# The recurrence's 128x128 transposes as 32x32 blocks on VectorE, moved into place by ScalarE, in a one-layer RWKV-7/Conformer step

## Chip, cores and metric

The kernel runs on one core of one Trainium2 chip. The metric is the device time of one execution in microseconds (us). The kernel before was run three times: median 1765.64 us, from 1764.25 to 1766.26. The profile is one more execution, 1765.73 us, of which 1763.5 us lie between its first and its last instruction (the span).

The five engines are called PE (TensorE; PEld is its weight load), DVE (VectorE), ACT (ScalarE), POOL (GpSimd) and SP (SyncE, which here only starts transfers). Each works through its own list of instructions in order.

## What is computed

One inference step of a hybrid decoder layer for 520 tokens (512 of one prompt, 8 single decode tokens), all in fp32. Cut to what matters:

```python
proj = rmsnorm(x, norm_g) @ w_in              # 2048 -> 3200 + 1024 + 2048 + 1024 + 4096 columns
r, k, v, ... = token_shift(proj)              # 16 heads of 64
def step(S, inp):                             # the recurrence, one token at a time
    sa = einsum('bhij,bhj->bhi', S, a_t)
    S = S * w_t + sa[..., None] * b_t + v_t[..., None] * k_t
    return S, einsum('bhij,bhj->bhi', S, r_t)
o = group_norm(scan(step)) + bonus
y_a = (o * silu(gate_a)) @ w_proj_a
y_b = (silu(layer_norm(conv31(glu))) * silu(gate_b)) @ w_proj_b
h = x + (sigmoid(ga) * y_a + sigmoid(gb) * y_b) @ w_out
h = h + sigmoid(h @ w_ple_gate) * (p @ w_ple)
y = rmsnorm(h, final_g)
```

## The kernel before

**The matrix products.** Activations lie as 128 channels by 520 tokens. Each weight and each activation is split into two fp32r parts, high and low, and a product is three matmuls (high-high, high-low, low-high), each in two halves of 260 tokens. `step` (L196 to L213) issues these six matmuls for one 128x128 weight. Weights are prepared in slabs of four such steps: ACT rounds the high part `wh` (L154, 128x512), DVE subtracts to get the low part `wl` (L67). Both have four buffers (`WB = 4`), and `step` asks for slabs up to three ahead (`AHEAD = 3`). So the rounding of slab k can start when PE has finished slab k-4, and PE needs it three slabs later. One slab is 24 matmuls.

**The order of the work.** The order on PE and DVE is the order in which the program issues. After each step, `tick` (L174) advances every running generator, and `yield n` means "go on n steps later". A generator that yields ROOM waits until a model of DVE's time (`work`, L95, with the charges of L103) has not run more than 1 us ahead of PE's. The order on ACT, POOL and SP is made at build time by a scheduler, which takes instructions as they become ready in its own model, in the order of issue where several are ready. Every engine then keeps its fixed order on the chip.

**The recurrence.** `wkv(p, box)` is a generator for head pair p, eight of them. Pair p+1 prepares its operands while pair p runs its scan. Its stages:

- `bk` (the decayed b and k of the pair) is multiplied with `ar`, giving the masked matrices `nba` and a part of `bn`. Then `bk` itself is transposed: 8 blocks of 128x128 in two groups of four, on PE against an identity (L548 to L551), and ACT copies each group of four out of PSUM into `bn` with one instruction.
- a 32x32 triangular inverse on DVE, whose blocks go into `ttb` (ACT, L615 and L617, 32 partitions each).
- `v` is transposed: four blocks on PE (L621 to L626), copied into `suv` by four ACT instructions. The scan starts from `suv`.
- the scan over eight chunks of 64 tokens. Each chunk has three groups of small matmuls on PE, `ly = 4` steps, one slab, apart: first `ar` x `suv` (called y here), copied by ACT to `xs` (L642); then `ttb` x `xs` (z), copied by ACT to `suv` (L648); then `bn` x `suv`, after which DVE computes the next chunk's `suv` and ACT scales it to `sf` (L662). Each group needs the copy behind the group before it.
- the group norm of the output `oc`; its normalised `on` is transposed, four blocks on PE (L693), and DVE multiplies straight out of PSUM into `og` (the buffer `bv`, L697), writing the pair's output.

**The end.** The last product is split into token halves. `finish` (L1050) sums the squares, takes root and reciprocal (`rf`), and multiplies all 16 blocks `h2[j]` by it, each group followed by its transfer to `y`. In the second half, which nothing follows, DVE multiplies 12 blocks in four instructions and POOL the blocks 12 to 15, one by one; transfers of DVE's groups are started by ACT, those of POOL's by SP.

Of the kernel before, what the change touches and what calls it, by code (L numbers as in the profile page):

```python
# [11 lines left out]
AF = mybir.ActivationFunctionType  # L12
ALU = mybir.AluOpType
# [4 lines left out]
P = 128  # L18
T = 520
NPR = 512  # L20
NS = 8
HF = T // 2
# [13 lines left out]


GROUPS = ([range(2 * _g, 2 * _g + 2) for _g in range(8)],
          [range(0, 1), range(12, 13), range(1, 4), range(4, 8), range(13, 16), range(8, 12)])
ON_POOL = (12, 13, 14, 15)  # L40


M_R, M_K, M_V, M_L, M_GA, M_GLA, M_GLB, M_GB, M_SA, M_SB = 0, 8, 16, 24, 25, 33, 41, 49, 57, 73
# [8 lines left out]
ROOM = -1  # L52
# [18 lines left out]
def body(nc, tc, a):  # L71
    with ExitStack() as es:
# [21 lines left out]
        act = nc.scalar.activation  # L94
        clock = {"pe": 0.0, "dve": 0.0}  # L95

        def work(us):
            clock["dve"] = max(clock["dve"], clock["pe"]) + us
# [1 line left out]
        def pe_work(name, n):  # L100
            clock["pe"] += 0.13 if n > 32 else 0.04

        vec = Paced(nc.vector, lambda name, n: work(0.0069 * n if name == "reciprocal" else (0.2 if name == "scalar_tensor_tensor" else 0.14) + 0.00107 * n))  # L103
        gps = Paced(nc.gpsimd, lambda name, n: work(0.0014 * n if n > 64 else 0.05))
        pe = Paced(nc.tensor, pe_work)

        def tt(eng, out, x, y, op):
            eng.tensor_tensor(out, x, y, op=op)
# [106 lines left out]
        def gemm(nk, xs, hs=(0, 1)):  # L215

            o = pm.tile([P, 2, 512], F32, name="mm")
            for k in range(nk):
                step(k, nk, xs[k], [o[:, h, :HF] for h in range(2)], hs)
                tick()  # L220
            return o[:, :, :HF] if len(hs) == 2 else o[:, hs[0], :HF]
# [6 lines left out]
        def half(h):  # L228
            return slice(64 * h, 64 * h + 64)

        def quarter(i):
            return slice(32 * i, 32 * i + 32)
# [19 lines left out]
        o = pa.tile([P, 512], F32, name="aux", tag="aux")  # L252
# [27 lines left out]
        ident = cst[:, C_ID:C_ID + P]  # L280
# [14 lines left out]
        def aux(name="aux"):  # L295
            return pa.tile([P, 512], F32, name=name, tag="aux")
# [43 lines left out]
        for i, n, o in ((0, 252, first[3][0]), (252, 252, first[3][1]), (504, 16, first[2][0])):  # L340
            o = o[:, HF:HF + n]
# [12 lines left out]
        def gt(name):  # L354
            return gp.tile([P, T], F32, name=name, tag="g")
# [71 lines left out]
        def wkv(p, box):  # L427
# [25 lines left out]
            for j, (out, off) in enumerate(((sg, O_W0), (av, O_A0))):  # L453
                for h in range(2):
                    hs = slice(h * HF, (h + 1) * HF)
                    o = aux()
# [45 lines left out]
            v = box["v"]  # L502
# [9 lines left out]
            bk = kq.tile([P, NCH, 2, 64], F32, name="bk")  # L512
# [16 lines left out]
            bn = bns[p % 2]  # L529
            f2 = lambda x: x.rearrange("p c a t -> p c (a t)")  # L530
            for c0 in (0, 4):
# [6 lines left out]
                for h in range(2):  # L538
                    s, u, o = half(h), half(1 - h), os[h]
                    mk = lambda s, i, n: gmask[s, i:i + n].unsqueeze(1).to_broadcast([64, 4, n])  # L540
                    tt(vec, nba[s, c0:c0 + 4], o[s, :, h * 64:h * 64 + 64], mk(s, 0, 64), ALU.mult)
                    i = 64 * (1 - h)
# [2 lines left out]
                    yield ROOM  # L545

            for c0 in (0, 4):
                o = aux().rearrange("p (c x) -> p c x", x=P)  # L548
                for c in range(4):
                    pe.transpose(o[:, c, :], f2(bk)[:, c0 + c, :], ident)  # L550
                act(bn[:, c0:c0 + 4].rearrange("p c h a x -> p c (h a) x")[:, :, 0::3, :],  # L551
                    o.rearrange("p c (h x) -> p c h x", h=2), AF.Copy)
                yield 2

            nd = dr.tile([2, NCH, 2, 32, 32], F32, name="nd", tag="nd", bufs=2)
            td = dr.tile([2, NCH, 2, 32, 32], F32, name="td", tag="td", bufs=2)
# [4 lines left out]
            o = aux()  # L561
# [31 lines left out]
            o = aux().rearrange("p (c x) -> p c x", x=64)  # L593
            for c in range(NCH):
                for h in range(2):
                    x, y = quarter(2 * h), quarter(2 * h + 1)
                    pe.matmul(o[y, c, 0:32], lhsT=nba[x, c, 32:64], rhs=dtt[x, c, :], start=True, stop=True)
            yt = kq.tile([P, NCH, 32], F32, name="yt")
            for h in range(2):
                y = quarter(2 * h + 1)  # L600
# [8 lines left out]
            o = aux().rearrange("p (c x) -> p c x", x=64)  # L609
            for c in range(NCH):  # L610
                for h in range(2):
                    x, y = quarter(2 * h), quarter(2 * h + 1)
# [5 lines left out]
            yield 2  # L618

            suv = kq.tile([P, 2, NCH, 64], F32, name="suv")  # L620
            o = aux().rearrange("p (w x) -> p w x", x=P)  # L621
            for w in range(4):
                pe.transpose(o[:, w, :], v[:, w * P:(w + 1) * P], ident)
            for e in range(2):
                for h in range(2):
                    act(suv[half(1 - h), h, e::2], o[half(e), :, h * 64:h * 64 + 64], AF.Copy)  # L626
            gps.memset(suv[0:64, 0, 0, :], 0.0)
            gps.memset(suv[64:128, 1, 0, :], 0.0)
            yield 6
# [3 lines left out]
            for c in range(NCH):  # L633
# [3 lines left out]
                y, z = yy[:, c % 2, 0], yy[:, c % 2, 1]  # L637
# [47 lines left out]
            on = gt("on")[:, :NPR].rearrange("p (c x) -> p c x", x=P)  # L685
# [3 lines left out]
                       m[half(1 - h), 1, e::2].unsqueeze(2).to_broadcast([64, 4, 64]), ALU.mult)  # L689
                yield ROOM  # L690
            yield 5
            ot = aux()
            for c in range(4):  # L693
                pe.transpose(ot[:, c * P:(c + 1) * P], on[:, c, :], ident)
            og = bv[:, :NPR]
            sl = box["sl"]
            yield 1  # L697
# [215 lines left out]
        for p in range(8):  # L913
# [7 lines left out]
            o = gemm(16, xn)  # L921
# [7 lines left out]
            o = gemm(16, xn)  # L929
# [4 lines left out]
            o = gemm(16, xn)  # L934
# [48 lines left out]
        def st(name):  # L983
            return sp2.tile([P, T], F32, name=name, tag="s")
# [11 lines left out]
        for j in range(KD):  # L996
            x = st("x")
# [12 lines left out]
        for k in range(2):  # L1010
            x = st("p")
# [4 lines left out]
        acc, rf = st("acc"), st("rf")  # L1016
        h2 = [hp.tile([P, 4, T], F32, name="h2") for _ in range(4)]
# [34 lines left out]
        def finish(h, sq):  # L1052
            t, sent = tok(h), [None, None]
            while flag["gated"] < LAST + (KD - LAST) * (h + 1):
                yield 1
            yield 4 * (1 - h)
            o = aux()
            nc.tensor.matmul(o[:, :HF], lhsT=one, rhs=acc[:, t], start=True, stop=False)
            nc.tensor.matmul(o[:, :HF], lhsT=one, rhs=sq[:, t], start=False, stop=True)  # L1059
            act(rf[:, t], o[:, :HF], AF.Sqrt, scale=1.0 / 2048, bias=eps[:, 0:1])  # L1060
            yield 14 * (1 - h)
            for i in range(0, HF, 130):
                r = rf[:, t][:, i:i + 130]
                vec.reciprocal(r, r)
                if h == 0:
                    yield ROOM
            for js in GROUPS[h]:

                if h and js[0] not in ON_POOL:
                    y = h2[js[0] // 4][:, js[0] % 4:js[-1] % 4 + 1, t]  # L1070
                    tt(vec, y, y, rf[:, t].unsqueeze(1).to_broadcast([P, len(js), HF]), ALU.mult)
                else:
                    for j in js:
                        y = h2[j // 4][:, j % 4, t]
                        tt(gps if h else vec, y, y, rf[:, t], ALU.mult)
                        if h == 0:
                            yield ROOM
                y = h2[js[0] // 4][:, js[0] % 4:js[-1] % 4 + 1, t]
                q = int(h == 1 and js[0] not in ON_POOL)
                with tc.issue_after(sent[q].ins) if h and sent[q] else ExitStack():  # L1080
                    sent[q] = (dma, nc.scalar.dma_start)[q](out=a["y"][js[0]:js[-1] + 1, :, t].rearrange("a p t -> p a t"), in_=y)

        flag["gated"] = 0
        order.enter_context(tc.manual_schedule(engines={mybir.EngineType.DVE}))
# [2 lines left out]
        for h in range(2):  # L1087
            for j in range(LAST, KD):
                sq = gate(j, (h,))
            start(finish(h, sq))  # L1090
# [74 lines left out]
```

## Time and profile before

| | us |
|---|---|
| median of three runs | 1765.64 |
| the profiled execution | 1765.73 |
| its span | 1763.5 |
| PE busy | 1746.3 |
| DVE busy | 1256.1 |
| ACT busy | 831.7 |
| POOL busy | 154.6 |

A row of a group of instructions reads: line, engine, operation, output <- inputs by the program's names (so `aux` is any PSUM scratch tile), shape, count | busy time, mean duration in ns of one | idle time of the engine just before them. A row of a timeline reads: start, duration, engine, line, operation, names, count. A row of the windows reads: stretch, length, then busy time of PE, PEld, DVE, ACT, POOL with counts, the granted PE clock as a share of full speed, the share of the DMA engines, GB/s. Matmuls overlap, and their ends are modelled; the pace of PE is read from starts.

### The profile page before, as it was taken

Reading aid. Unit: us, or ns where it says so; the run is one execution under the profiler, and the core shown is the slowest. Engines: PE = TensorE matmul, PEld = TensorE weight load, DVE = VectorE, ACT = ScalarE, POOL = GpSimd, SP = SyncE. Lnnn points to the kernel's source line nnn. Section 1 sums busy time; section 2 is a strip of 40 time slices with the busy share of each in tenths; the row PEclk is TensorE's granted clock in tenths of the full one; section 3 lists DMA queues with packets and bytes.
Section 4 is the critical chain, followed back from the end, with each engine's and each line's share of the span. In section 5 each row is a group of like instructions: output and inputs, shape, how many; then the busy total and the mean of one; then the engine's idle time right before and its main releaser. Section 6 shows DMA issues by size and latency. Waiting matters only on the chain.

```text
span 1763.5 us, 36946 instructions
## 1 busy us (share of the span) xinstructions
PE 1746.3 (99%) x15064; PEld 1736.0 (98%) x15064; DVE 1256.1 (71%) x2411; ACT 831.7 (47%) x1644; POOL 154.6 (9%) x205
## 2 busy tenths in 40 slices
PE   9999999999999999999999999999999999999996
PEld 9999999999999999999999999999999999999996
DVE  7578889889888898888898998577344333334557
ACT  6734546456455464474564433455233222243344
POOL 1100100001001001000010000002022000001111
PEclk9999999999999999999999999999999999999998
DMA  7252333333333433334324444568455332353333
GB/s 231 88 128 91 95 115 98 97 109 100 121 92 85 127 100 97 109 93 110 108 86 115 144 133 151 172 223 271 153 186 181 121 110 95 98 190 96 96 100 106
DMA packets 122186, 221.34 MB, mean 126 GB/s; under 512 B 48017, under 2 KB 57361, under 8 KB 122017
## 3 DMA queue, kind: packets, MB, share of 16 engines
q1 hardware_dynamic: 120416, 217.39, 39.9%
q8 instruction: 118, 1.93, 0.5%
q10 hardware_dynamic: 1600, 1.60, 0.3%
q14 instruction: 52, 0.42, 0.1%
HBM read 189.61 MB, written 29.34 MB: 124 GB/s over the span
## 4 chain that ended last, share of the span: by engine, by line
PE 97%; DVE 1%; DMA 1%; ACT 0%; POOL 0%; issue 0%; SPq 0%; POOLq 0%; DVEq 0%; ACTq 0%
PE mm L211 89%; PE aux L67 7%; PE aux L211 1%; DMA w<-in_win 0%; DVE h L67 0%; DMA x<-in_xT 0%; POOL h L67 0%; DVE wl L67 0%; DVE c L67 0%; DVE rf L67 0%; PE aux L1059 0%; POOLq L1161 0%; SPq L143 0%; ACT wh L154 0%; ACT ttb L615 0%
## 5 line engine op out<-in xcount | busy, mean ns | idle before, releaser
L154 ACT ACTIVATE wh<-w 128x512 fp32r<-128x512 f32 (+1 forms) x541 | 338.9, 628 | 603.4 <-PE mm L211 529.3
L211 PE MATMUL mm<-xh,wh 128*128 128x260 f32 x2784 | 581.8, 290 | 0.6 <-ACT xh L266 0.4
L211 PE MATMUL mm<-xh,wl 128*128 128x260 f32 x2784 | 561.1, 283 | 0.0
L211 PE MATMUL mm<-xl,wh 128*128 128x260 f32 x2784 | 560.1, 282 | 0.3 <-DVE xl L67 0.3
L67 DVE TENSOR_TENSOR wl<-w,wh 128x512 fp32r<-128x512 f32 (+1 forms) x541 | 373.3, 692 | 166.0 <-ACT wh L154 163.3
L211 PEld LDWEIGHTS mm<-xh,wh 128*128 128x128 f32 x2784 | 428.1, 189 | 3.9 <-ACT wh L154 0.7
L211 PEld LDWEIGHTS mm<-xl,wh 128*128 128x128 f32 x2784 | 428.4, 188 | 0.6 <-DVE xl L67 0.5
L211 PEld LDWEIGHTS mm<-xh,wl 128*128 128x128 f32 x2784 | 427.8, 188 | 0.1
L211 PE MATMUL mm<-hi,wl 128*128 128x260 f32 x1600 | 332.8, 283 | 0.0
L211 PE MATMUL mm<-hi,wh 128*128 128x260 f32 x1600 | 332.5, 283 | 0.0
L211 PE MATMUL mm<-lo,wh 128*128 128x260 f32 x1600 | 331.8, 282 | 0.0
L211 PEld LDWEIGHTS mm<-hi,wh 128*128 128x128 f32 x1600 | 251.4, 189 | 0.0
L211 PEld LDWEIGHTS mm<-lo,wh 128*128 128x128 f32 x1600 | 251.1, 188 | 0.0
L211 PEld LDWEIGHTS mm<-hi,wl 128*128 128x128 f32 x1600 | 250.1, 188 | 0.0
L67 DVE SCALAR_TENSOR_TENSOR c<-u,prm,c 128x482 f32<-128x482 f32 (+14 forms) x240 | 180.2, 751 | 4.3
L67 DVE TENSOR_REDUCE ti<-tm 128x8 f32<-128x16 f32 (+30 forms) x248 | 73.6, 297 | 8.5
L67 DVE TENSOR_TENSOR p<-mm,rs 128x520 f32<-128x520 f32 x78 | 54.2, 695 | 33.2 <-PE mm L211 32.3
L67 DVE TENSOR_TENSOR tm<-ti,ni 128x16 f32<-128x16 f32 (+30 forms) x248 | 73.7, 297 | 4.9
L67 DVE TENSOR_TENSOR s<-mm,s 128x520 f32<-128x520 f32 x32 | 22.4, 699 | 54.6 <-PE mm L211 54.6
L662 ACT ACTIVATE sf<-suv,epl 64x64 f32<-64x64 f32 x112 | 38.7, 345 | 43.9 <-DVE suv L67 42.3
L67 POOL TENSOR_TENSOR sq<-hi,lo 128x520 f32<-128x520 f32 (+1 forms) x20 | 26.8, 1344 | 353.6 <-DVE one L67 184.0
L67 DVE SCALAR_TENSOR_TENSOR suv<-aux,epl,sf 64x64 f32<-64x64 f32 x96 | 27.2, 283 | 38.5 <-ACT wh L154 19.4
(232 smaller groups left out, 1576.4 us busy)
## 6 DMA issues: line engine op xcount, KB each, us to landing
w<-in_win SPq DMA_DIRECT2D x170, 512.0 KB, 3.7
w<-in_wout SPq DMA_DIRECT2D x32, 512.0 KB, 3.8
w<-in_wpg SPq DMA_DIRECT2D x24, 512.0 KB, 3.6
s<-sga_d SPq DMA_DIRECT2D x32, 260.0 KB, 3.7
w<-in_wpa SPq DMA_DIRECT2D x16, 512.0 KB, 3.8
w<-in_wpb SPq DMA_DIRECT2D x16, 512.0 KB, 3.8
wx<-in_wpg SPq DMA_DIRECT2D x32, 256.0 KB, 3.8
x<-in_xT SPq DMA_DIRECT2D x16, 260.5 KB, 6.1
```

What stands on the lines that cost most here:

```text
L67: return f(*args, **kw)
L154: behind.append(act(wh[:, k], w[:, k], AF.Copy))
L211: nc.tensor.matmul(o[h], lhsT=w[:, used[0] % 4, :], rhs=x[:, h * HF:(h + 1) * HF], start=(k == 0 and i == 0), stop=(k == nk - 1 and i == 2))
L662: act(sf[half(h)], suv[half(h), h, c + 1, :], AF.Copy, scale=epl[half(h), c + 1:c + 2])
```

## The change

All three PE transposes of the recurrence go. In their place one DVE instruction transposes the 32x32 blocks of a 128x512 tile each within its own place, and ACT moves the blocks to where a 128x128 transpose has them: 16 copies of 32 partitions x 4 x 32 for each of the two groups of `bk` (before: one ACT copy of 128x512 each), 8 copies of 32x256 for `v` (before: four of 64x256), 16 copies of 32x4x32 for `on` (before: none). The outputs of the block transposes and the moved `on` are new tiles of the pool `gp`. The last scaling runs on DVE alone, in wider instructions, and the charges that the order is made with change: wide DVE instructions are charged less (0.07 us + 1.04 ns an element instead of 0.14 us + 1.07 ns), `scalar_tensor_tensor` more. The file is one line shorter at the top, so L67 before is L66 after.

```diff
 GROUPS = (...,
-          [range(0, 1), range(12, 13), range(1, 4), range(4, 8), range(13, 16), range(8, 12)])
-ON_POOL = (12, 13, 14, 15)
+          [range(0, 1), range(1, 4), range(4, 8), range(8, 12), range(12, 14), range(14, 15), range(15, 16)])
...
-        vec = Paced(nc.vector, lambda name, n: work(0.0069 * n if name == "reciprocal" else (0.2 if name == "scalar_tensor_tensor" else 0.14) + 0.00107 * n))
+        vec = Paced(nc.vector, lambda name, n: work(0.0069 * n if name == "reciprocal" else (0.25 if name == "scalar_tensor_tensor" else 0.07 if n > 250 else 0.14) + 0.00104 * n))
...
             for c0 in (0, 4):
-                o = aux().rearrange("p (c x) -> p c x", x=P)
-                for c in range(4):
-                    pe.transpose(o[:, c, :], f2(bk)[:, c0 + c, :], ident)
-                act(bn[:, c0:c0 + 4].rearrange("p c h a x -> p c (h a) x")[:, :, 0::3, :],
-                    o.rearrange("p c (h x) -> p c h x", h=2), AF.Copy)
-                yield 2
+                o = gt("bkt")[:, :NPR].rearrange("p (c x) -> p c x", x=P)
+                yield ROOM
+                vec.transpose(o, f2(bk)[:, c0:c0 + 4, :])
+                for i in range(4):
+                    for j in range(4):
+                        act(bn[quarter(j), c0:c0 + 4, i // 2, i // 2, 32 * (i % 2):32 * (i % 2) + 32],
+                            o[quarter(i), :, quarter(j)], AF.Copy)
...
-            o = aux().rearrange("p (w x) -> p w x", x=P)
-            for w in range(4):
-                pe.transpose(o[:, w, :], v[:, w * P:(w + 1) * P], ident)
-            for e in range(2):
-                for h in range(2):
-                    act(suv[half(1 - h), h, e::2], o[half(e), :, h * 64:h * 64 + 64], AF.Copy)
+            o = gt("vt")[:, :NPR]
+            yield ROOM
+            vec.transpose(o, v[:, :NPR])
+            o = o.rearrange("p (c e q) -> p c e q", e=2, q=32)
+            for i in range(4):
+                for e in range(2):
+                    act(suv[quarter(2 * (1 - i // 2) + e), i // 2, :, 32 * (i % 2):32 * (i % 2) + 32], o[quarter(i), :, e, :], AF.Copy)
...
-            ot = aux()
-            for c in range(4):
-                pe.transpose(ot[:, c * P:(c + 1) * P], on[:, c, :], ident)
+            on2, ot = gt("ont")[:, :NPR], gt("ot")[:, :NPR]
+            yield ROOM
+            vec.transpose(on2, on.rearrange("p c x -> p (c x)"))
+            for i in range(4):
+                for j in range(4):
+                    act(ot[quarter(j)].rearrange("p (c x) -> p c x", x=P)[:, :, quarter(i)],
+                        on2[quarter(i)].rearrange("p (c x) -> p c x", x=P)[:, :, quarter(j)], AF.Copy)
+            yield 2
...
-            for js in GROUPS[h]:
-
-                if h and js[0] not in ON_POOL:
-                    ...
-                else:
-                    for j in js:
-                        y = h2[j // 4][:, j % 4, t]
-                        tt(gps if h else vec, y, y, rf[:, t], ALU.mult)
-                        ...
+            for n, js in enumerate(GROUPS[h]):
                 y = h2[js[0] // 4][:, js[0] % 4:js[-1] % 4 + 1, t]
-                q = int(h == 1 and js[0] not in ON_POOL)
+                tt(vec, y, y, rf[:, t].unsqueeze(1).to_broadcast([P, len(js), HF]), ALU.mult)
+                q = n % 2 * h
```

What it moves on ACT, at two places where the scan of one pair meets the preparation of another. The first is the middle of pair 0's scan (`suv`, `sf`, `xs` are its copies, `bn_786` belongs to pair 1, `st` is a small copy, `sg` a sigmoid). Before:

```order
L648 ACTIVATE suv<-aux 64x64 x2
L395 ACTIVATE sg<-p 128x520
L154 ACTIVATE wh<-w 128x512
L662 ACTIVATE sf<-suv,epl 64x64 x2
L154 ACTIVATE wh<-w 128x512
L642 ACTIVATE xs<-aux 64x64 x2
L551 ACTIVATE bn_786<-aux 128x4x2x64
L154 ACTIVATE wh<-w 128x512
L648 ACTIVATE suv<-aux 64x64 x2
L551 ACTIVATE bn_786<-aux 128x4x2x64
L564 ACTIVATE st<-aux 48x128
L154 ACTIVATE wh<-w 128x512
```

Now, at the same place:

```order
L649 ACTIVATE suv<-aux 64x64 x2
L153 ACTIVATE wh<-w 128x512
L663 ACTIVATE sf<-suv,epl 64x64 x2
L552 ACTIVATE bn_786<-bkt 32x4x32 x32
L564 ACTIVATE st<-aux 48x128
L394 ACTIVATE sg<-p 128x520
L153 ACTIVATE wh<-w 128x512
L643 ACTIVATE xs<-aux 64x64 x2
L153 ACTIVATE wh<-w 128x512
L649 ACTIVATE suv<-aux 64x64 x2
```

The two wide copies, which stood apart with the scan's copies between them, have become 32 small ones in one piece, ahead of the next `xs` and the next `wh`. In pairs 0, 1, 2 and 5 the 32 stand in one piece, in pairs 3, 4, 6 and 7 in two pieces of 16 with one or two rows of the scan between them.

The second place is the start of pair 5's scan, on ACT, now (`ot` is pair 4's output, `suv` with `xs` behind it is where pair 5's scan starts, ACT_TABLE_LOAD changes the function table):

```order
L153 ACTIVATE wh<-w 128x512
L615 ACTIVATE ttb<-tm 32x8x32 x4
L698 ACTIVATE ot<-ont 32x4x32 x16
L617 ACTIVATE ttb<-aux 32x8x32
L458 ACTIVATE a<-aux,prm 128x260 x2
L617 ACTIVATE ttb<-aux 32x8x32
L153 ACTIVATE wh<-w 128x512
L480 ACT_TABLE_LOAD
L480 ACTIVATE sp<-sig 128x8
L627 ACTIVATE suv<-vt 32x8x32 x8
L153 ACTIVATE wh<-w 128x512
L643 ACTIVATE xs<-aux 64x64 x2
```

Before, the row of `ot` isn't there, and `suv` is four copies. The scan's first matmul waits for the last of the eight `suv` copies, and so for the sixteen `ot` copies ahead of them.

The third is DVE where pair 1's output is transposed, now (`bv<-ot` reads what ACT's sixteen copies wrote):

```order
L66 TENSOR_TENSOR wl<-w,wh 128x512
L66 SCALAR_TENSOR_TENSOR r<-p,omu,q 128x520
L66 STREAM_TRANSPOSE ont<-on 128x512
L66 TENSOR_TENSOR wl<-w,wh 128x512
L66 SCALAR_TENSOR_TENSOR bv<-ot,prm,bv 128x512
L66 TENSOR_TENSOR bv<-bv,sl 128x512
L66 SCALAR_TENSOR_TENSOR cs<-cst,sig 128x256 x2
```

Before, `bv` read PE's transpose out of PSUM there. Now a wait for ACT stands between two rows of DVE that are one slab apart.

More of the change, by code (lines that the diff above doesn't have):

```diff
@@ L1066, in finish @@
                     yield ROOM
-            for js in GROUPS[h]:
-                if h and js[0] not in ON_POOL:
-                    y = h2[js[0] // 4][:, js[0] % 4:js[-1] % 4 + 1, t]
-                    tt(vec, y, y, rf[:, t].unsqueeze(1).to_broadcast([P, len(js), HF]), ALU.mult)
-                else:
-                    for j in js:
-                        y = h2[j // 4][:, j % 4, t]
-                        tt(gps if h else vec, y, y, rf[:, t], ALU.mult)
-                        if h == 0:
-                            yield ROOM
+            for n, js in enumerate(GROUPS[h]):
                 y = h2[js[0] // 4][:, js[0] % 4:js[-1] % 4 + 1, t]
-                q = int(h == 1 and js[0] not in ON_POOL)
+                tt(vec, y, y, rf[:, t].unsqueeze(1).to_broadcast([P, len(js), HF]), ALU.mult)
+                q = n % 2 * h
                 with tc.issue_after(sent[q].ins) if h and sent[q] else ExitStack():
                     sent[q] = (dma, nc.scalar.dma_start)[q](out=a["y"][js[0]:js[-1] + 1, :, t].rearrange("a p t -> p a t"), in_=y)
+                if h == 0:
+                    yield ROOM
         flag["gated"] = 0
```

## Prediction

> **What bounds the kernel now.** I read the page first, then the windows, the waits, the groups by shape, and the timeline where pair 0 transposes.
>
> ```profile
> span 1763.5 us, 36946 instructions
> PE 1746.3 (99%) x15064; PEld 1736.0 (98%) x15064; DVE 1256.1 (71%) x2411; ACT 831.7 (47%) x1644; POOL 154.6 (9%) x205
> 620.00:800.00 180.00, 180.00 (x1624) 178.75 (x1623) 161.81 (x333) 104.38 (x218) 15.18 (x33) 1.00 0.33 100
> ACT wh L154 <- PE mm L211: 545.5, 342, 5.4
> ```
>
> PE is busy from end to end, so a microsecond of PE work removed is a microsecond of the kernel, and a microsecond in which PE waits is lost. In the recurrence's stretch (620 to 800) DVE is at 90% (161.81 of 180), ACT at 58% (104.38). The last row says why PE doesn't wait: it is ACT that waits for PE, 342 times, with the next `wh` as soon as PE frees a buffer. So ACT goes in step with PE, three slabs ahead, and its free time lies between its rows, never in one piece.
>
> **What PE is rid of.** The steps around pair 0's first four transposes:
>
> ```profile
> 122.17 0.40 PE L211 MATMUL mm<-xh,wh 128*128 128x260 f32 x2
> ...
> 122.90 0.40 PE L211 MATMUL mm<-xh,wh 128*128 128x260 f32 x2
> ...
> 123.62 0.60 PE L67 MATMUL aux<-cst,bk 128*128 128x128 f32 x4
> 123.98 0.48 PE L211 MATMUL mm<-xh,wh 128*128 128x260 f32 x2
> ...
> 124.79 0.40 PE L211 MATMUL mm<-xh,wh 128*128 128x260 f32 x2
> L67 PE MATMUL aux<-cst,bk 128*128 128x128 f32 x64 | 9.6, 272 | 0.0
> L67 PE MATMUL aux<-cst,on 128*128 128x128 f32 x32 | 4.8, 272 | 0.0
> L67 PE MATMUL aux<-cst,v 128*128 128x128 f32 x32 | 4.8, 272 | 0.0
> ```
>
> A step without transposes takes 122.90 - 122.17 = 0.73 us. The one with them takes 123.98 - 122.90 = 1.08, and the next 124.79 - 123.98 = 0.81. Four transposes thus cost 0.35 + 0.08 = 0.43 us. There are 64 + 32 + 32 = 128, 32 groups of four: 32 x 0.43 = **-13.8 us**, all of it on the bound engine.
>
> **What ACT gets.** The groups of ACT by shape, and a piece of its timeline:
>
> ```profile
> L154 ACT ACTIVATE wh<-w 128x512 fp32r<-128x512 f32 x539 | 338.0, 629 | 602.8 <-PE mm L211 529.3 <-DMA w<-in_win 40.1 <-PE aux L211 12.3
> L662 ACT ACTIVATE sf<-suv,epl 64x64 f32<-64x64 f32 x112 | 38.7, 345 | 43.9 <-DVE suv L67 42.3
> L459 ACT ACTIVATE a<-aux,prm 128x260 f32<-128x260 f32 x16 | 6.8, 474 | 0.1
> L617 ACT ACTIVATE ttb<-aux 32x256 f32<-32x256 f32 x16 | 6.0, 375 | 1.4 <-PE aux L67 1.2
> L395 ACT ACT_TABLE_LOAD x9 | 11.5, 1283 | 2.3 <-DVE p L67 2.3
> L642 ACT ACTIVATE xs<-aux 64x64 f32<-64x64 f32 x128 | 28.0, 218 | 25.5 <-PE aux L67 23.9
> L615 ACT ACTIVATE ttb<-tm 32x256 f32<-32x256 f32 x32 | 13.2, 414 | 4.1 <-DVE tm L67 3.7
> L626 ACT ACTIVATE suv<-aux 64x256 f32<-64x256 f32 x32 | 12.1, 380 | 4.7 <-PE aux L67 4.1
> L551 ACT ACTIVATE bn<-aux 128x512 f32<-128x512 f32 x16 | 9.6, 600 | 13.0 <-PE aux L67 12.9
> L395 ACT ACTIVATE sg<-p 128x520 f32<-128x520 f32 x16 | 10.2, 640 | 2.1 <-DVE p L67 1.9
> L564 ACT ACTIVATE st<-aux 48x128 f32<-48x128 f32 x8 | 2.2, 269 | 4.7 <-PE aux L67 4.7
> 186.17 1.70 ACT L615 ACTIVATE ttb<-tm 32x256 f32<-32x256 f32 x4 [0.35 <-DVE tm L67]
> ...
> 189.84 0.64 ACT L927 ACTIVATE p<-p 128x520 f32<-128x520 f32 x1
> 190.38 0.61 ACT L154 ACTIVATE wh<-w 128x512 fp32r<-128x512 f32 x1
> ```
>
> ACT's time goes by elements per partition, not by partitions: SBUF to SBUF, 256 elements on 32 partitions take 414 ns, 512 on 128 take 629, so 0.84 ns an element, and a 32x4x32 copy (128 elements) takes an estimated 414 - 107 = 307 ns. Does a copy start before the one ahead has ended? `wh` at 190.38 starts 0.10 us before `p` ends (190.48). But four `ttb` copies, which are what the new ones are (32 partitions, the next going to other partitions), take 1.70, so 0.425 each against 0.414 of one: no overlap. I take 0.32 us a copy, 0.43 for the 32x256 ones; with overlap it would be 0.21 and 0.33. So 16 copies are 5.1 us, 32 are 10.2, the eight of `v` 3.4, where before stood 2 x 0.60 for `bk`, 1.6 for `v`, nothing for `on`. Per pair ACT gets 10.2 + 3.4 + 5.1 - 2.8 = 15.9 us more, 127 in all, which it has in sum, but not in one piece.
>
> The Trainium skill ("ScalarE: Activation LUTs", What ACT_TABLE_LOAD costs) says that back-to-back ACTIVATEs overlap by about 93 ns. The trace agrees for `p` and `wh` (0.10) and disagrees for `ttb`; by the rule the copies would be at the 0.21 above.
>
> **What waits for those pieces.** One slab of PE with the scan's matmuls, from the chain (the first and the last of four in a row), and DVE's part of the scan:
>
> ```profile
> 240.95 2.93 PE mm L211 x24
> ...
> 250.69 2.94 PE mm L211 x24
> L67 DVE SCALAR_TENSOR_TENSOR suv<-aux,epl,sf 64x64 f32<-64x64 f32 x96 | 27.2, 283 | 38.5 <-ACT wh L154 19.4 <-PE aux L67 17.5
> ```
>
> A slab is (250.69 - 240.95)/3 = 3.25 us. The scan's groups are one slab apart, so a copy may come 3.25 us after its matmul, `xs` 6.5 us after the `bn` matmul of the chunk before. Take the first order shown (pair 1's `bn`). PE's `bn` group of pair 0 is time 0. DVE's two `suv` (0.57) and two block transposes (0.7 each, below), while ACT does `sf`, and 0.2 to pass between engines put the start of the 32 copies at 2.2. Then 10.24 + 0.28 (`st`) + 0.64 (`sg`) + 0.63 (`wh`) + 0.45 (`xs`) = 12.24, plus 0.15 to reach PE: 14.6. PE wants `xs` at 6.5 and waits **8.1 us**. The other places go the same way; where a `wh` row stands ahead, the copies start 0.65 us after PE has freed its buffer:
>
> - pair 2 (32, ahead of `xs` 3 slabs on): 1.3 + 12.3 + 0.15 - 9.75 = 4.0; pair 5: 0.65 + 12.3 + 0.15 - 2.25 x 3.25 = 5.8; pair 6: 0.65 + 12.3 + 0.15 - 2.75 x 3.25 = 4.2.
> - pair 4 (16, `xs`, 16, `suv`): 0.65 + 5.1 + 0.45 + 0.15 - 1.25 x 3.25 = 2.3, then 5.1 + 0.28 + 0.64 + 0.63 + 0.45 - 3.25 = 3.9; pair 7 likewise 2.0 and 3.2, pair 3 1.5 and 1.3; pair 0 none, no scan runs and the `wh` behind comes just in time.
> - where `ot` and the copies of `v` stand ahead of a scan's start, pairs 1, 3, 5, 7: 4.1, 2.7, 6.2, 1.9. Pair 5 is the second order shown: from the first `wh` 1.7 + 5.1 + 0.38 + 0.86 + 0.38 + 0.63 + 1.3 + 0.2 + 3.4 = 14.0 us to the last `suv` against 2.45 slabs, 8.0 us.
>
> Sum 8.1 + 14.0 + 14.2 + 14.9 = **+51 us**; with 0.21 and 0.33 us a copy the same list gives 19.
>
> **The clock.** Waits of this length did not exist before, but the end shows one:
>
> ```profile
> 1748.00:1749.00 1.00, 0.00 (x0) 0.00 (x0) 0.86 (x4) 0.85 (x2) 0.00 (x0) 1.00 1.05 341
> 1749.00:1750.00 1.00, 0.52 (x1) 0.50 (x2) 0.42 (x1) 0.51 (x1) 0.00 (x0) 0.71 0.99 354
> 1750.00:1751.00 1.00, 0.71 (x2) 0.00 (x0) 0.00 (x0) 0.25 (x1) 0.00 (x0) 0.50 0.09 30
> L254 PE MATMUL aux<-zero x14: 397/422/423, 1.2 to 4.0; 128*128 128x260 bf16 x14
> ```
>
> After some 2 us without matmuls the granted clock falls to 0.50. How long it stays there once work resumes, only the start shows: 14 matmuls in 1.2 to 4.0, 0.215 us each, where full pace is 2.93/24 = 0.122. So a wait of over 2 us can cost up to half of some 4 us again, 2.1 us. Seven waits of 3.5 us and more: 0 to 15 us, I take the middle, **+7**. The Trainium skill ("TensorE: Matmul & The Clock Gate", Part 1) has the clock halved after an idle window of about 3.4 us and back after a busy one; nothing above leans on it.
>
> **DVE and the end.** The 32 block transposes come on top of DVE:
>
> ```profile
> L67 DVE STREAM_TRANSPOSE tm<-ti x8: 387/438/445, 185.7 to 998.9; 128x256 f32<-128x256 f32 x8
> 1745.28 2.81 DVE L67 TENSOR_TENSOR h<-h,rf 128x260 f32<-128x260 f32 x8
> 1748.00 0.43 DVE L67 TENSOR_TENSOR s<-s,h 128x260 f32<-128x260 f32 x1
> 1746.96 0.39 ACT L1025 ACTIVATE s<-mm 128x260 f32<-128x260 f32 x1 [2.29 <-PE mm L211]
> 1753.08 5.22 DVE L67 TENSOR_TENSOR h<-h,rf 128x260 f32<-128x260 f32 x4
> 1753.19 5.70 POOL L67 TENSOR_TENSOR h<-h,rf 128x260 f32<-128x260 f32 x4 [15.93 <-DVE rf L67]
> ```
>
> One of 128x512 should take 0.44 to 0.88 us, I take 0.7: 2.8 us a pair, on an engine with 18 of 180 free. It fits; it costs nothing while DVE's rows between slabs stay inside a slab. At the end, `s` started at 1748.00 although ACT's half was there at 1747.35: eight products of the first half stood ahead. Three wide ones now stand there, so the chain starts up to 0.6 us sooner. Then DVE does 16 blocks at 2.81/8 = 0.35 each, 5.6 us, in place of POOL's end 5.8 after 1753.08: 0.2. Together **-0.8**; from +0.5 (two queues with other last transfers) to -2.
>
> **Sum.** Span and the 2.2 us around it make the profiled 1765.73, within 0.1 of the median: 1765.7 - 13.8 - 0.8 + 51 + 7 = **1809**.
>
> **Rivals.**
> - *The copies overlap.* Then 19 us of waits, only four over 2 us: 1765.7 - 14.6 + 19 = 1770, with few clock losses. For it: the pair `p`, `wh`. Against it: `ttb`, the same kind of copy, doesn't. 1770 is at the edge of what this measurement tells from no change (0.2%, 3.5 us). It is the case that the overlap rule of the Trainium skill ("ScalarE: Activation LUTs") would give.
> - *Faster: the transposes' 14 us stay, the copies hide.* Needs both the overlap and starts about 1 us sooner than I set them at the eleven places, 19 - 9 or less: 1751 to 1761, say 1756. For it: ACT is only 58% busy and DVE delivers the blocks early. Against it: each piece stands behind a `wh` or `sf` that can't come sooner, because it waits for PE. It turns where the list's waits come to less than 14.6 us, which with starts as I set them is at 0.19 us a copy.
> - *DVE becomes a bound as well.* `bv<-ot` (third order shown) waits for 16 copies, 5.1 us, but was issued three steps, 2.2 us, after the transpose: some 2.8 us in which DVE stands, with `wl` and the scan's `suv` queued behind, 8 x 2.8 = 22 us that an engine at 92% does not win back: 1809 + 22 = 1831. For it: DVE's 90%, and wide instructions charged less. Against it: while PE waits, DVE catches up.
>
> **How the numbers follow.** The forecast has 0.60: the `ttb` row is the nearest there is. Overlap 0.15 (0.09 slower, 0.06 within 0.2%), faster 0.14, DVE 0.11. Slower 0.60 + 0.09 + 0.11 = 0.80, same 0.06, faster 0.14. The range takes in the overlap case and its spread, from 1762, and up to the DVE case, 1832: out of it lie the faster case and the upper half of the DVE case, 0.2.
>
> **What would show it.** Right: copies of 0.31 us that start 0.32 apart; PE idle before `aux<-xs,ttb`, `aux<-suv,bn` and `aux<-suv,ar`, released by ACT, some 50 us in about a dozen waits, the longest near pair 1's `bn`; granted clock under 1 behind them; the matmuls on `cst` gone. Wrong: PE without idle time between 50 and 1700 us, or copies 0.21 apart; waits of PE that DVE ends would be the last rival.

## The result, and the profile after

| | us |
|---|---|
| before, four runs | 1765.84 (1764.25 to 1766.26) |
| changed, four runs | 1846.17 (1842.82 to 1846.31) |
| ratio | 1.0456, interval 1.0443 to 1.0468 |
| profiled execution of the changed kernel | 1842.82, span 1841.0 |

The kernel became 4.6% slower. The forecast was 1809, so the direction was right, and the size was too small by 37 us: above the range. The page of the changed kernel, its span, busy times and chain:

```profile
span 1841.0 us, 37109 instructions
PE 1763.0 (96%) x14936; PEld 1746.8 (95%) x14936; DVE 1275.5 (69%) x2438; ACT 952.2 (52%) x2043; POOL 144.6 (8%) x201
PE 74%; ACT 11%; DVE 10%; issue 2%; DMA 2%; SPq 0%; DVEq 0%; ACTq 0%
```

PE was busy 99% and is busy 96%. Two things are in these rows. Time in which PE is not busy is 1841.0 - 1763.0 = 78.0 us, where it was 17.2. And PE's busy time *rose* by 16.7 us, although 128 matmuls are gone: the same matmuls took longer. What PE waited for, in the changed kernel (total us, times, longest):

```profile
PE aux L66 <- ACT oc L645: 17.8, 5, 5.6
PE aux L66 <- ACT xs L643: 14.6, 3, 7.2
PE aux L66 <- ACT suv L627: 8.8, 8, 1.3
PE mm L210 <- DVE wl L66: 7.1, 3, 4.2
PE aux L66 <- ACT suv L649: 6.8, 3, 3.6
```

The copies that the scan needs (`oc` stands right behind `xs`) end most of it. The new instructions cost what the prediction had for them: 0.7 us a block transpose on DVE, 307 and 415 ns a copy on ACT.

```profile
L66 DVE STREAM_TRANSPOSE bkt<-bk x16: 659/695/711, 121.3 to 1003.3; 128x512 f32<-128x512 f32 x16
L552 ACT ACTIVATE bn<-bkt 32x128 f32<-32x128 f32 x256 | 78.7, 308 | 4.7 <-DVE bkt L66 1.7
L698 ACT ACTIVATE ot<-ont 32x128 f32<-32x128 f32 x128 | 39.3, 307 | 4.6 <-DVE ont L66 3.2
L627 ACT ACTIVATE suv<-vt 32x256 f32<-32x256 f32 x64 | 26.5, 415 | 3.1 <-DVE vt L66 2.2
```

The place of the first order in the section on the change, pair 1's `bn`: first ACT, then PE at the same time, then the windows there (the third column from the end is PE's granted clock: 0.86, 0.50, 0.72, 1.00).

```profile
216.29 10.20 ACT L552 ACTIVATE bn<-bkt 32x128 f32<-32x128 f32 x32 [0.35 <-DVE bkt L66]
...
227.35 0.61 ACT L153 ACTIVATE wh<-w 128x512 fp32r<-128x512 f32 x1
227.87 0.43 ACT L643 ACTIVATE xs<-aux 64x64 f32<-64x64 f32 x2
```

```profile
219.33 0.40 PE L210 MATMUL mm<-xh,wl 128*128 128x260 f32 x2
219.57 0.40 PE L210 MATMUL mm<-xh,wh 128*128 128x260 f32 x2
...
228.35 0.69 PE L66 MATMUL aux<-xs,ttb 128*128 128x64 f32 x2 [7.18 <-ACT xs L643]
228.80 0.78 PE L210 MATMUL mm<-xh,wh 128*128 128x260 f32 x2
229.38 0.64 PE L210 MATMUL mm<-xl,wh 128*128 128x260 f32 x2
229.81 0.64 PE L210 MATMUL mm<-xh,wl 128*128 128x260 f32 x2
```

```profile
224.00:225.00 1.00, 0.00 (x0) 0.00 (x0) 0.00 (x0) 0.96 (x4) 0.00 (x0) 0.86 0.00 0
...
230.00:231.00 1.00, 1.00 (x7) 1.00 (x6) 0.93 (x3) 0.00 (x0) 0.00 (x0) 0.50 0.40 146
231.00:232.00 1.00, 1.00 (x8) 1.00 (x8) 0.96 (x2) 0.00 (x0) 0.00 (x0) 0.72 0.43 103
232.00:233.00 1.00, 1.00 (x11) 1.00 (x10) 0.95 (x2) 0.63 (x1) 0.00 (x0) 1.00 0.94 319
```

The 32 copies run without a gap, 10.20/32 = 0.319 us apart. PE has nothing to do for 7.18 us. Meanwhile the granted clock falls to half at 224.7, and it stays there until 231.6: PE works again from 228.35, but two matmuls then take 0.43 us (229.81 - 229.38) where they took 0.24 (219.57 - 219.33). So a part of the wait is paid a second time: by an estimate from these rows (231.6 - 228.35) x (1 - 0.24/0.43) = 1.4 us on top of the 7.18.

### The profile page after: what moved, and what is told of

Read it like the earlier page. It is cut to its first block, busy times and chain, and to the rows that moved or that the text cites. A ratio compares the mean times of both kernels' runs of the same rounds, so it can differ in the third digit from the quotient of the medians.

```text
span 1841.0 us, 37109 instructions
## 1 busy us (share of the span) xinstructions
PE 1763.0 (96%) x14936; PEld 1746.8 (95%) x14936; DVE 1275.5 (69%) x2438; ACT 952.2 (52%) x2043; POOL 144.6 (8%) x201
## 3 DMA queue, kind: packets, MB, share of 16 engines
q10 hardware_dynamic: 1072, 1.07, 0.2%
## 4 chain that ended last, share of the span: by engine, by line
PE 74%; ACT 11%; DVE 10%; issue 2%; DMA 2%; SPq 0%; DVEq 0%; ACTq 0%
PE mm L210 68%; PE aux L66 5%; ACT bn L552 4%; ACT ot L698 2%; DVE wl L66 2%; ACT suv L627 1%; PE aux L210 1%; DVE c L66 1%; DVE tm L66 1%; DMA w<-in_win 1%; DVE ti L66 1%; ACT wh L153 1%; DVE p L66 1%; DVE on L66 0%; DVE h L66 0%
## 5 line engine op out<-in xcount | busy, mean ns | idle before, releaser
L210 PE MATMUL mm<-xh,wh 128*128 128x260 f32 x2784 | 588.5, 293 | 0.3 <-ACT wh L153 0.3
L210 PE MATMUL mm<-xh,wl 128*128 128x260 f32 x2784 | 569.1, 286 | 7.3 <-DVE wl L66 7.1
L210 PE MATMUL mm<-xl,wh 128*128 128x260 f32 x2784 | 568.4, 286 | 0.3 <-DVE xl L66 0.3
L66 DVE TENSOR_TENSOR wl<-w,wh 128x512 fp32r<-128x512 f32 (+1 forms) x541 | 377.8, 700 | 208.1 <-ACT wh L153 206.1
L210 PEld LDWEIGHTS mm<-xh,wl 128*128 128x128 f32 x2784 | 436.2, 192 | 8.5 <-DVE wl L66 8.5
L210 PEld LDWEIGHTS mm<-xh,wh 128*128 128x128 f32 x2784 | 437.2, 193 | 3.8 <-ACT wh L153 1.0
L210 PEld LDWEIGHTS mm<-xl,wh 128*128 128x128 f32 x2784 | 437.1, 192 | 0.6 <-DVE xl L66 0.5
L66 DVE SCALAR_TENSOR_TENSOR c<-u,prm,c 128x482 f32<-128x482 f32 (+14 forms) x240 | 177.2, 738 | 4.0
L552 ACT ACTIVATE bn<-bkt 32x128 f32<-32x128 f32 x256 | 78.7, 308 | 4.7 <-DVE bkt L66 1.7
L66 DVE TENSOR_REDUCE ti<-tm 128x8 f32<-128x16 f32 (+30 forms) x248 | 73.6, 297 | 8.6
L66 DVE TENSOR_TENSOR tm<-ti,ni 128x16 f32<-128x16 f32 (+30 forms) x248 | 75.7, 305 | 5.4
L66 DVE TENSOR_TENSOR p<-mm,rs 128x520 f32<-128x520 f32 x78 | 54.0, 692 | 32.0 <-PE mm L210 31.0
L66 DVE TENSOR_TENSOR s<-mm,s 128x520 f32<-128x520 f32 x32 | 22.4, 700 | 56.7 <-PE mm L210 56.7
L66 POOL TENSOR_TENSOR sq<-hi,lo 128x520 f32<-128x520 f32 (+1 forms) x20 | 26.8, 1343 | 353.7 <-DVE one L66 184.0
```

The costliest lines, as they stand in the source:

```text
L66: return f(*args, **kw)
L210: nc.tensor.matmul(o[h], lhsT=w[:, used[0] % 4, :], rhs=x[:, h * HF:(h + 1) * HF], start=(k == 0 and i == 0), stop=(k == nk - 1 and i == 2))
L552: act(bn[quarter(j), c0:c0 + 4, i // 2, i // 2, 32 * (i % 2):32 * (i % 2) + 32], o[quarter(i), :, quarter(j)], AF.Copy)
```

## Experiments

The theory after the result: pieces of small copies on ACT stand ahead of copies that PE waits for, and behind each wait the clock is at half speed for some microseconds. Rivals: DVE, with 32 transposes and another order, is what comes late; the other charges spoil the order; moving the blocks costs whoever does it.

### Wide copies in place of the small ones

The block transposes stay, the blocks aren't moved: `bk` and `v` get their wide copies of before, scaled by zero, `on` one of 128x512.

```diff
-                for i in range(4):
-                    for j in range(4):
-                        act(bn[quarter(j), ...], o[quarter(i), :, quarter(j)], AF.Copy)
+                act(bn[:, c0:c0 + 4]..., o.rearrange(...), AF.Copy, scale=0.0)
...
```

> The changed kernel with its block transposes on VectorE, but with the small copies replaced by as many ScalarE copies as the kernel before had, plus one of 128x512 for the output. What it leaves out: the blocks are not moved into place, and the copies of bk and v write zeros. Theory (pieces of small copies keep PE waiting, and the clock halves behind each wait): PE waits under 6 us between 50 and 1250 us, no half-clock stretch there, and the time is the one before less the 13.8 us of transposes and some 2 us at the end: 1750, from 1745 to 1757. Rival (VectorE with 32 more transposes, a denser order and more tiles in its pool holds PE): 1800 or more, with waits that VectorE ends.

Measured: 1752.47 us, ratio 0.9928 (0.9914 to 0.9941). Page and waits of PE:

```profile
span 1750.0 us, 36728 instructions
PE 1734.2 (99%) x14936; PEld 1723.1 (98%) x14936; DVE 1273.6 (73%) x2438; ACT 839.1 (48%) x1652; POOL 149.3 (9%) x201
PE aux L1061 <- DVE sq L66: 1.2, 1, 1.2
```

DVE does all the block transposes here, at 73%, and the longest wait of PE is the one behind the last product. So DVE's work isn't what costs, and without the small copies the change would gain 13 us. This kernel also splits the loss, since it differs from the changed one in the copies alone, and PE issues the same 14936 matmuls in the same order. The spans differ by 1841.0 - 1750.0 = 91.0 us: PE's idle time is 78.0 against 15.8, **62.2 us of waits**, and its busy time 1763.0 against 1734.2, **28.8 us of slower matmuls**.

### Bk's part, and the part of v and on

Two kernels: the changed one with the transposes and wide copies of `bk` back as before, and its complement, with those of `v` and `on` back. The first:

```diff
-                vec.transpose(o, f2(bk)[:, c0:c0 + 4, :])
+                for c in range(4):
+                    pe.transpose(o[:, c, :], f2(bk)[:, c0 + c, :], ident)
...
```

The second, and likewise for `on`:

```diff
-            vec.transpose(o, v[:, :NPR])
+            for w in range(4):
+                pe.transpose(o[:, w, :], v[:, w * P:(w + 1) * P], ident)
...
```

> The changed kernel, with the transposes of bk back on PE and their two wide copies. Those of v and on stay as block transposes on DVE with small copies on ACT. My theory (each piece of small copies keeps PE waiting, and the clock halves behind the wait): the waits behind the bk pieces (33.7 us of PE idle time in the changed kernel) and the six half-speed stretches behind them go, those at the scans' starts (some 27 us, six stretches, 3.4 or 6.8 us each, half of which is lost: some 13 us) stay. 1765.7 - 6.9 (v and on off PE) - 2 (end) + 27 + 13 = 1797, from 1785 to 1805. Rival, waits only, without a price of the clock: 1784. Rival, the loss comes from bk alone, since only there 32 copies stand in a piece: about 1757.

> The complement: bk as in the changed kernel (DVE transposes, 32 small copies a pair), v and on back on PE. My theory: idle time of PE before the matmuls of the scan behind the bk pieces, 34 us, with six or seven half-speed stretches, some 13 us lost; 1765.7 - 6.9 (bk off PE) - 2 (end) + 34 + 13 = 1804, from 1792 to 1812. Rival, waits only, no price of the clock: 1791. Rival, the pieces of different places make each other worse (one piece alone is caught up by the three slabs that ACT is ahead): under 1780.

Measured: 1799.74 us with `bk` on PE (ratio 1.0196, 1.0182 to 1.0210), 1812.19 with `bk` alone on DVE and ACT (1.0266, 1.0252 to 1.0281). What PE waited for, first in the one, then in the other:

```profile
PE aux L66 <- ACT suv L626: 22.0, 13, 4.1
```

```profile
PE aux L66 <- ACT xs L642: 16.7, 3, 7.1
PE aux L66 <- ACT suv L648: 14.9, 3, 6.9
PE aux L66 <- ACT oc L644: 8.3, 3, 6.4
```

With `bk` on PE the waits are at the scans' starts, for the copies of `v` (with those of `on` ahead of them). With `bk` alone they are behind its pieces, the three rows above with 39.9 us in all. Each has six stretches at half clock in the recurrence, as the theory had it, and 1784 and 1791, the values without a price of the clock, are ruled out (the second would be 1797 with its own 39.9 us of waits). The second came out 8 us above my 1804, at the upper end of its range: its order puts the 32 copies in one piece at pairs 4, 6 and 7 too, where the changed kernel had two, and its waits are 6 us longer than the 34 that I had taken over. Both parts lose more than they save. Nor does `bk` alone make the loss, or only the meeting of the parts: against the kernel before they lose 34.9 and 47.4 us, together 82.3, where the whole change lost 80.3.

### The same copies in another order

At all three places the loops change places:

```diff
-                for i in range(4):
-                    for j in range(4):
+                for j in range(4):
+                    for i in range(4):
...
```

> The changed kernel with the two loops over blocks exchanged, so that four copies in a row (two for v) write from the same partition on; instructions and their places in ScalarE's list stay the same. Theory: a copy starts before the one ahead has ended only when both write from the same partition on, so a piece of 16 takes 4 x 0.32 + 12 x 0.21 = 3.8 us instead of 5.1; the list of waits goes from 51 to 26 us by the same sums, the measured 61 to about 33, and the half-clock stretches from 12 to about 8: 1802, from 1792 to 1815. Rival (the copies are not what PE waits for, or do not overlap): 1840 to 1850.

Measured: 1845.81 us, ratio 1.0457 (1.0441 to 1.0473): no change. The copies stand as far apart as before.

```profile
216.30 10.20 ACT L552 ACTIVATE bn<-bkt 32x128 f32<-32x128 f32 x32 [0.35 <-DVE bkt L66]
```

Keeping the output partitions is not enough to make copies overlap. The input still changes its partitions from one to the next, so I tried pairs that keep both:

```diff
             for c0 in (0, 4):
                 ...
                 vec.transpose(o2[-1], f2(bk)[:, c0:c0 + 4, :])
+            for i in range(4):
+                for j in range(4):
+                    for c0 in (0, 4):
+                        act(bn[quarter(j), c0:c0 + 4, ...], o2[c0 // 4][quarter(i), :, quarter(j)], AF.Copy)
```

> The changed kernel with both block transposes of bk ahead of the copies, and the two copies that have the same partitions in and out (one of each group) one behind the other. If copies overlap when they keep to the same partitions (as oc behind xs seems to do), every second copy starts 0.21 us behind the one ahead, a piece of 32 takes 8.4 us in place of 10.2, and the time falls by 8 to 14 us, to about 1834. If small copies never overlap: 0.318 apart, 10.2 a piece, and 1842 to 1850.

Measured, by one execution: 1837.49 us, 8.7 below the changed kernel, near the lower end of what overlap should give. The changed kernel's own executions lie up to 3.5 us apart, so the length of the piece says more than the time:

```profile
216.88 8.64 ACT L554 ACTIVATE bn<-bkt 32x128 f32<-32x128 f32 x32 [0.34 <-DVE bkt L66]
```

8.64/32 = 0.270 us a copy in place of 0.319: about what one has if every second copy starts 0.10 us early. The starts in the trace say the same: 0.21 to 0.22 us apart inside a pair, 0.30 from one pair to the next. So a copy of this kind overlaps with the one ahead if it has the same partitions in and out. Of the copies that move blocks between quarters only such pairs do.

### Copies a few at a time

The loops of the swapped kernel, but the program goes a step on behind each copy of `v` and `on`, and `bk`'s copies are made by generators of their own, one of each group every second step.

```diff
+                def move(o=o, c0=c0, bn=bn):
                     for j in range(4):
                         for i in range(4):
                             act(bn[quarter(j), ...], o[quarter(i), :, quarter(j)], AF.Copy)
+                            yield 2
+                start(move())
```

> The changed kernel with the exchanged loops and the same copies issued a few at a time: bk's by a generator of its own, one of each group every second step, v's and on's one a step. All work as in the changed kernel, nothing left out. Theory: pieces of at most 12 copies (3 us) with the scan's rows between: PE waits 0 to 12 us, 0 to 4 half-clock stretches: 1758, from 1748 to 1775. Rival VectorE: 1800 or more, since its work is the same.

Measured: 1769.01 us, ratio 1.0021 (1.0012 to 1.0030). The same transposes and the same 448 copies, only issued apart, and 77 of the 80 us are gone. What stays is waits where ACT has no room, here with pair 5's `bn`:

```profile
708.14 0.63 ACT L153 ACTIVATE wh<-w 128x512 fp32r<-128x512 f32 x1
708.80 2.22 ACT L553 ACTIVATE bn<-bkt 32x128 f32<-32x128 f32 x7
711.03 0.45 ACT L647 ACTIVATE xs<-aux 64x64 f32<-64x64 f32 x2
```

Nor have the rows ahead of these any idle time before them; `xs` comes 2.2 us late for PE.

I then tried to do better with fewer copies, `bk` on PE again, and `v` and `on` (two copies a step) or `on` alone (one a step) spread:

> bk back on PE, the new last scaling and charges, and the small copies of v and on issued few at a time (the program goes a step on after every two copies). My theory (only copies in a piece ahead of the scan's copies cost): 1765.7 - 6.9 - 2, and some 4 us of waits where the copies of v stand ahead of a scan's start: 1761, from 1757 to 1766, no half-speed stretch, or one. Rival, the small copies of v and on cost PE what they cost with bk on PE and in pieces, however they are issued: about 1795.

> Only on by DVE and small copies, one copy a step; bk and v on PE as before, new last scaling and charges. My theory: 1765.7 - 3.4 - 2 and 1 to 3 us of waits: 1762, from 1759 to 1765. Rival, DVE comes late, since bv waits for sixteen copies spread over twelve us: waits of PE that DVE ends, over 1770.

Measured: 1783.07 us (ratio 1.0102, 1.0088 to 1.0116) and 1777.31 (1.0072, 1.0058 to 1.0086). Both lie over 12 us above the ranges that I had given. The rival's time for the second (over 1770) came out, but not its sign: of the waits of PE only one of 0.52 us is ended by DVE. ACT in the second, where pair 1's scan begins, ahead of a wait of PE of 2.64 us:

```profile
298.58 2.23 ACT L696 ACTIVATE ot<-ont 32x128 f32<-32x128 f32 x7 [0.22 <-DVE ont L66]
300.83 1.28 ACT L394 ACT_TABLE_LOAD   x1
302.13 0.64 ACT L394 ACTIVATE sg<-p 128x520 f32<-128x520 f32 x1
302.67 0.70 ACT L661 ACTIVATE sf<-suv,epl 64x64 f32<-64x64 f32 x2
303.40 0.63 ACT L153 ACTIVATE wh<-w 128x512 fp32r<-128x512 f32 x1
304.06 0.45 ACT L641 ACTIVATE xs<-aux 64x64 f32<-64x64 f32 x2
304.52 1.58 ACT L696 ACTIVATE ot<-ont 32x128 f32<-32x128 f32 x5
306.12 0.63 ACT L153 ACTIVATE wh<-w 128x512 fp32r<-128x512 f32 x1
306.78 1.26 ACT L696 ACTIVATE ot<-ont 32x128 f32<-32x128 f32 x4
```

From 298.58 to 308.04 ACT is never idle: 5.07 us of copies, a table load, and its usual rows. That it is busy only 49% in the whole says nothing about these 10 us. "Only pieces cost" was too simple: copies cost where ACT has less free time than they take before the next row that PE wants, whether in one piece or in three. The kernel that spreads everything is faster than these two, but not because PE waits less: by the pages PE is idle 27.7 us in it, and 31.0 and 26.8 in these. PE is busy 1739.5 us in it and 1749.8 and 1748.7 in these, since all 128 transposes are off PE there. Why its 448 copies cost no more waits than 192 and 128 here stays open. A part may be that copies issued apart need not run apart: in the first of these two the scheduler put the eight copies of `v` in one piece of 3.42 us in four of the eight pairs, where the kernel that spreads everything has at most five together.

### The charges, and the last scaling, alone

Both are the kernel before with one part of the diff, as it stands in the section on the change.

> The kernel before with only the charges of the order changed. Theory: the order moves by a few rows, PE goes on without waits: 1766, within 4 us. Rival (the denser order on VectorE is part of the loss): 5 to 40 us slower, with waits that VectorE ends.

> The kernel before, with the new last scaling alone. By the two traces the time from the last product to the end of the span fell from 16.1 to 14.2 us: 1763.8, from 1763.0 to 1765.0. Rival: the end is the same and the difference was one execution's: 1765.7.

Measured: 1765.84 us with the charges (ratio 1.0004, 0.9995 to 1.0012) and 1763.41 with the scaling (0.9991, 0.9982 to 1.0000). The charges do nothing. The scaling gains some 1.4 us, at the edge of what can be told from none.

### Other movers: SP's transfers, POOL

The first kernel moves the blocks of all three places by transfers; the second those of `bk` and `on` with `nc.gpsimd.tensor_copy` in the same way, and `v` is on PE as before.

```diff
-                        act(bn[quarter(j), ...], o[quarter(i), :, quarter(j)], AF.Copy)
+                        dma(out=bn[quarter(j), ...], in_=o[quarter(i), :, quarter(j)])
...
```

> The changed kernel, with every small copy of ACT turned into a transfer from SBUF to SBUF on SP's queue (56 transfers a pair, 128 bytes a row); DVE's block transposes, tiles and charges as they are. My theory, that it is ACT's pieces which PE waits for: PE's waits for ACT go, the clock stays at 1.00 in the recurrence; 1765.7 - 13.8 - 2 = 1750 if the transfers land in time, up to 1775 if the weights queued behind them on SP, or bv behind ot on DVE, come late. Rival, that blocks moved later than by PE cost the same whoever moves them: over 1800, with waits of PE for SP's queue in place of those for ACT.

> bk and on by block transposes on DVE as in the changed kernel, their small copies made by POOL instead of ACT, bv seven steps later behind the sixteen copies of on; v on PE as before; new last scaling and charges. My theory (the loss came from the place of the copies on ACT, among the rows that PE waits for): POOL is busy 9% and none of its rows stands between the scan's matmuls, so PE doesn't wait and the clock stays at 1.00: 1765.7 - 10.3 (24 groups of four transposes off PE) - 2 = 1753, from 1751 to 1762. Rival: POOL's copies are slow (no row of before has such a copy; its 128x8 copies take 0.23 to 0.71 us), and what stands behind a piece of 32 on POOL (q, nsh), and DVE behind that, comes late: over 1770, with waits of PE that DVE ends.

Measured: 1997.13 us by transfers (ratio 1.1316, 1.1296 to 1.1336), 1811.81 by POOL (1.0267, 1.0253 to 1.0281). My theory's times were wrong both times, and the rivals' came out. By transfers two things cost. Blocks come late: of PE's 186 us of waits up to 1250 us, 48 end with the blocks of `v` themselves, and another 41 follow a stand of DVE at `bv`, which waits for the blocks of `on`. The rest mostly follow transfers that stand behind the blocks in SP's queue. By POOL no wait of PE ends with the blocks, and what stands behind them is what comes late. SP in the first, then ACT there:

```profile
122.14 21.46 SPq L552 DMA_DIRECT2D bn<-bkt  x32
```

```profile
150.37 1.15 ACT L153 ACTIVATE wh<-w 128x512 fp32r<-128x512 f32 x2 [21.44 <-DMA w<-in_win]
```

Starting one such transfer takes SP 21.46/32 = 0.67 us, and the next weights stand behind all 32: ACT waits 21.44 us for them, and PE waits 12.09 us for that `wh`. In the second kernel POOL, SP, ACT and PE, one behind the other:

```profile
217.26 17.71 POOL L552 COPY bn<-bkt 32x128 f32<-32x128 f32 x32 [13.14 <-DVE bkt L66]
235.05 1.28 POOL L66 TENSOR_TENSOR gb<-p,sg 128x520 f32<-128x520 f32 x1
```

```profile
236.35 0.34 SPq L943 DMA_DIRECT2D gb_d<-gb  x1
236.73 0.93 SPq L142 DMA_DIRECT2D w<-in_win  x2
```

```profile
241.19 1.15 ACT L153 ACTIVATE wh<-w 128x512 fp32r<-128x512 f32 x2 [11.76 <-DMA w<-in_win]
```

```profile
242.79 1.12 PE L66 MATMUL aux<-suv,ar 128*128 128x64 f32 x4 [7.59 <-DVE suv L66]
```

POOL's `gb` stands behind 17.71 us of copies, `gb`'s transfer waits for it on SP, the weights stand behind that transfer, `wh` behind the weights, DVE's `suv` behind its `wl`, and PE waits 7.59 us. POOL is busy 17% in this kernel. The mover's share of busy time doesn't decide it: in each queue something stands behind the piece that PE needs within three slabs, 9.75 us.

## Why the prediction fell short

**PE's saving: right to within 2 us.** -13.8 was worked out for 128 transposes. With wide copies PE's busy time fell by 1746.3 - 1734.2 = 12.1, and the span by 13.5, which has the gain at the end in it.

**Cost and spacing of the copies: right.** 0.32 and 0.43 us forecast, 0.319 and 0.415 measured; no overlap, as the `ttb` row said. The rival of overlapping copies falls for this order of copies. The Trainium skill ("ScalarE: Activation LUTs", What ACT_TABLE_LOAD costs) says that back-to-back ACTIVATEs overlap by about 93 ns; the runs show it only for copies that keep their partitions (0.270 us on average in pairs, 0.319 else).

**The list of waits behind `bk`: right.** Forecast and measured, in us, each measured as PE's idle time before the matmul: pair 1 8.1 and 7.2, pair 2 4.0 and 4.1, pair 3 1.5 + 1.3 and 1.4 + 1.2, pair 4 2.3 + 3.9 and 1.9 + 3.6, pair 5 5.8 and 5.6, pair 6 4.2 and 5.1, pair 7 2.0 + 3.2 and 1.9 + 1.8. Sum 36.3 and 33.7. The 0.2 and 0.15 us for passing work from engine to engine stand on no row; in the changed kernel the waiting matmul starts 0.05 to 0.14 us behind the copy that it needs.

**The waits at the scans' starts: too small.** Forecast 14.9, for pairs 1, 3, 5 and 7; measured about 27. Pair 1 had 5.5 for 4.1, pair 3 6.2 for 2.7, pair 5 4.2 for 6.2, pair 7 2.3 for 1.9. Places that the list didn't have make the rest, the greatest at pair 2, where it is DVE that waits for the sixteen `ot` copies. DVE in the changed kernel, with the wait behind it on PE:

```profile
425.90 0.75 DVE L66 SCALAR_TENSOR_TENSOR bv<-ot,prm,bv 128x512 f32<-128x512 f32 x1 [5.47 <-ACT ot L698]
```

```profile
431.14 0.80 PE L210 MATMUL mm<-xh,wl 128*128 128x260 f32 x2 [4.22 <-DVE wl L66]
```

This is the mechanism of the last rival. `bv` made DVE stand 28.4 us in the eight pairs, more than the 22 of the rival, but DVE won most of it back: PE waited 7.1 us in all for DVE's `wl`, 2.2 of them among the 6.2 of pair 3.

**The clock: the step that failed.** "0 to 15 us, I take the middle, +7", from seven waits of 3.5 us and more, at up to 2.1 us each. The matmuls lost 28.8 us. PE issues the same matmuls in the kernel with wide copies, so the loss can be placed matmul by matmul: 22.7 us lie in the stretches at half clock, where 50.1 us of work takes 27.4 with wide copies. Another 4.9 lie at full clock beside the waits: the last matmul before a wait reads 0.28 us where it read 0.12 with the next one right behind it, and the first behind a wait reads 0.1 us more. The sum had no term for these. About 1 us is scattered.

Both factors of the clock's term were too small. Not seven but twelve stretches at half clock lie in the recurrence, since shorter waits set them off too: pair 7's 1.87 us, or 0.92 and 1.31 close together. And a stretch cost 22.7/12 = 1.9 us, where the +7 has 1.0 a wait. The trace's record of the granted clock has each stretch 3.41 or 6.83 us long, six of either, 61 us; PE was at work in 50 of them. The "end" row that I had taken as a bound shows how soon the clock falls, not how long it stays down once work is back, and I had set that from the start of the program alone. The Trainium skill ("TensorE: Matmul & The Clock Gate", Part 1) has the clock judged in windows of 3413 ns that run on by themselves. The lengths agree; had I taken whole windows as the price, seven waits at 3.41 x 0.44 to 6.83 x 0.44 would have been an estimated 11 to 21 us (0.44 is 1 - 0.24/0.43, from the rows behind pair 1's wait).

The traces also show what sets a stretch off. In each of the ten that have such stretches in the recurrence, all falls and rises of the clock there stand on marks 3.41 us apart. I set PE's idle time in each interval between two marks, up to 1250 us, beside the clock in the next. The clock fell behind 78 intervals, 77 of them with 1.68 us of idle time or more and one with 1.34. It stayed up behind no interval with more than 1.88. It rose again only behind intervals with at most 0.46. So what counts is how much of one interval is idle, here about half of it, and not the length of a wait alone. A wait of 1.94 us inside one interval set a stretch off (the kernel with `bk` on PE, 312.11). One of 2.02 us with a mark in its middle did not (by POOL, 433.95), nor one of 1.41 (`v` and `on` spread, 311.73). The Trainium skill ("TensorE: Matmul & The Clock Gate", Part 1) has the clock at half after at least one idle window; here about half of one was enough.

**The end: small.** -0.8 forecast; the scaling alone gave 1.4 between medians, and 2.3 between two spans, 1763.5 and 1761.2.

So of the 37 us missing, 16 are the clock's (22.7 against 7), 6 the matmuls that read longer outside of its stretches, and 11 the waits' (62.2 against 51). The rest comes from the saving with the end, 13.5 for 14.6, and from the median of the four runs, which lies 3 us above the profiled execution.

No run was made to vary the idle share of an interval on purpose; the bounds above are those of this kernel's waits.

## What to carry to other kernels

Before moving work to an engine with free time, read on its queue what stands behind the place where the work lands and when the bound engine wants that: an engine that is 47% busy had no 10 us to give, and neither had one at 9%. Price a wait of PE twice: once for its length, and, if it leaves about half of a 3.4 us interval idle, once for the half-speed stretch behind it (here 1.9 us each). A 128x128 transpose made of 32x32 blocks is paid for in moving the blocks: four cost PE 0.43 us, but DVE 0.70 and ACT 5.1.

## What the hardware showed that was not expected

- In the recurrence the half clock came in stretches of 3.41, 6.83 and, by transfers, up to 17.07 us: always whole multiples of 3.41, on fixed marks. About half an interval of idle time was enough to set one off.
- ACT's copies of 32x4x32 overlapped by about 0.10 us only where both input and output stay on the same partitions as in the copy ahead.
- Starting a transfer of 32x4x32 from SBUF to SBUF holds SP for about 0.6 us, where the start of 512 KB of weights takes 0.37 in the same kernel; it is the number of starts that costs.
- POOL's copy of 32x4x32 takes 448 ns, 1.5 times ACT's, and 32 in a row 17.71 us (0.55 each).
